# The seven products of a channel mixer: weights split in another order, additions moved between engines, and a reordered start

## The chip, the cores and the metric

The kernel runs on one core of a Trainium2 chip. The metric is the device time of one execution in microseconds; the median of several executions stands for a kernel. The engines are named as in the profile: PE is TensorE with its weight load PEld, DVE is VectorE, ACT is ScalarE, POOL is GpSimd, and SP is the engine whose queue issues most of the transfers.

## The reference, cut to what matters

Two layers work on a latent stream of 1024 tokens of width 1024. Layer 0 mixes tokens by a chunked gating, layer 1 by windowed attention, and each layer ends in a channel mixer with a convolution over the tokens:

```
def conv_ffn(h, w_up, conv_w, conv_b, w_down):          # h 1024 x 1024, w_up 1024 x 5632
    a, b = jnp.split(h @ w_up, 2, axis=-1)
    ap = jnp.pad(a, ((0, 0), (1, 1), (0, 0)))
    a = ap[:, :-2] * conv_w[0] + ap[:, 1:-1] * conv_w[1] + ap[:, 2:] * conv_w[2] + conv_b
    return (jax.nn.gelu(a) * b) @ w_down
...
        # last sublayer of layer i; sh2, sc2, g2 = columns of silu_c @ ada_w[i] + ada_b[i]
        h = modulate(rms_norm(x, norm_g[i, 2]), sh2, sc2)
        x = x + g2 * rms_norm(conv_ffn(h, f_w_up[i], f_conv_w[i], f_conv_b[i], f_w_down[i]), norm_g[i, 3])
```

All is float32. The change bears on the channel mixer of layer 1 and on the attention output that runs into it.

## The kernel before, in words

**One program, fixed orders.** The kernel is one program under a scheduler that fixes each engine's order of instructions when it is built. Work that belongs to different steps is mixed by Python generators: `step(gen)` lets a generator emit its next piece at that place in the program, and `tick()` does so for the norms that are pending.

**Split operands.** A float32 operand enters PE as two fp32r parts: ACT casts the source (tags `wh` for weights, `cmb` or `ah` for activations), and DVE subtracts the cast from the source (`wl`, `al`). One product of two operands is three matmuls: hi with hi, hi with lo, lo with hi. The tags `wh` and `wl` are rings of four buffers of 1024 columns, and `raw`, into which weights are loaded, is a ring of three. A buffer of a ring is written again only when its last reader has ended.

**The up-projection of layer 1** (`lat_ffn`, about 2237 to 2765 us of the trace). A job computes 128 columns f of the branch a and the same of b. It needs two weight blocks, `wa` and `wb`, each halved along the input channels: b11 and b21 are the halves of `wa`, b12 and b22 those of `wb`. The activations, in pairs of half-width groups (a11, a12, a21, a22), have been combined and split beforehand by `combine`. A job then has seven products instead of eight, with sums of weights t1 = b12 - b11, t2 = b22 - t1, t3 = b22 - b12 and t4 = b21 - t2, in three banks (X, Y, Z) of the product memory, in this order:

```
X  = a11 b11         -> s1 copied by ACT
Y  = s2 t2           -> b1 copied by ACT, then b1 + s1
Z  = s1 t1           -> s5 copied by ACT, then s5 + s1
Y += s3 t3           -> b2 copied by ACT        (Y holds s2 t2 + s3 t3)
X += a12 b21         -> left half of a copied by ACT
Z += s4 b22          -> DVE adds to b2 and b1
Y += a22 t4          -> right half of a, added by DVE
```

Y is used three times, so its fourth product (s3 t3) waits for the copy of b1 out of it. Below, P1 to P7 are these products in order. In a "full" job a product is 12 matmuls of 512 columns, in a "half" job (group g1) 12 of 256. After P7 `conv_gate` works on the finished job while PE is in the next: the first tap (POOL, `TENSOR_SCALAR row<-row,cwcols,lncols`), two more taps (DVE, `SCALAR_TENSOR_TENSOR row<-row,cwcols,row`), Gelu (ACT, `ACTIVATE row<-row`), a product with b, and the store.

Five "plain" jobs, which use only the first 512 tokens, come first, while the last two tiles of attention output are still being finished (`last_o`: eight weight blocks of `w_o`, 96 matmuls, then `late_norm` and transposes). Then come 17 full jobs with a half job after each third. During one job, `weights` loads, sums and splits the blocks of the next, one piece at each `step(more)`. A steady generator (`ada_steps`, one step after each full or half job) accumulates the gate of the sublayer in `lacc`, and its ninth step splits `lacc`, multiplies it by ones on PE in four matmuls and adds the bias.

The recording helper gives nearly every instruction of the trace the line L50, so rows are told apart by their tiles: `row` is a ring of work rows, `psA` and `psB` are product banks, `ident` the identity matrix of the transposes.

Of the kernel before, what the change touches and what calls it, by code (L numbers as in the profile page):

```python
# [15 lines left out]
P = 128  # L16
# [16 lines left out]
def hybrid_kernel(  # L33
# [79 lines left out]
    def psB(shape=(P, 512)):  # L113
        return ps.tile(list(shape), F32, name=nm("psB"), tag="psB", bufs=4)
# [71 lines left out]
    def ada_steps(l, m, streams, space=None):  # L186
# [11 lines left out]
        if m in (2, 5):  # L198
# [3 lines left out]
            for s, acc in zip(streams, accs):  # L202
                g = t_gate()
                hi, lo = (t_row(F32R), t_row(F32R)) if space else (t_w("wh"), t_w("wl"))
                S.copy(hi, acc)
                V.tensor_sub(lo, acc, hi)
                for h in range(2):
                    hs = slice(h * 512, (h + 1) * 512)
                    p = psB()
                    T.matmul(p, ones_r, hi[:, hs], start=True, stop=False)  # L210
                    T.matmul(p, ones_r, lo[:, hs], start=False, stop=True)
                    V.tensor_tensor(out=g[:, hs], in0=p, in1=bb[:, hs], op=ALU.add)
                V.tensor_tensor(out=g, in0=g, in1=ng, op=ALU.mult)
                gates[(l, m, s)] = g
# [682 lines left out]
    def lat_ffn(l, stage, n0, halos, gate, between, later):  # L897
# [60 lines left out]
        def weights(f, out, plain):  # L958
# [5 lines left out]
            def pair(src, names):  # L964
                n = src.shape[-1]
                hi, lo = t_w("wh"), t_w("wl")
                split_into((hi[:, 0:n], lo[:, 0:n]), src)
                for i, name in enumerate(names):
                    out[name] = [t[:, i * 512:(i + 1) * 512].rearrange("p (k n) -> p k n", n=P) for t in (hi, lo)]

            if plain:
                pair(wa, ("b11", "b21"))
                yield
                pair(wb, ("b12", "b22"))
                yield
                return
# [3 lines left out]
            pair(wa, ("b11", "b21"))  # L980
            yield
            G.tensor_tensor(out=t1, in0=b12, in1=b11, op=ALU.subtract)
            G.tensor_tensor(out=t2, in0=b22, in1=t1, op=ALU.subtract)
            V.tensor_sub(t4, b21, t2)
            pair(t24[:, 0:1024], ("t2", "t4"))
            yield
            G.tensor_tensor(out=t3, in0=b22, in1=b12, op=ALU.subtract)
            pair(t13[:, 0:1024], ("t1", "t3"))
            yield
            pair(b22, ("b22",))  # L990
# [4 lines left out]
        def conv_gate(f, a, N, b, where):  # L995
            c = t_row()[:, 0:N]
            G.tensor_scalar(out=c, in0=a[:, 1:1 + N], scalar1=cw[:, NF + f:NF + f + 1], scalar2=cb[:, f:f + 1],
                            op0=ALU.mult, op1=ALU.add)
# [46 lines left out]
        def up(f, groups, nxt):  # L1045
# [20 lines left out]
            def wide(t):  # L1066
                return t.rearrange("p (g n) -> p g n", n=256)

            X, Y, Z = psB(), psB(), psB()
            product(X, "a11", "b11", True)  # L1070
# [6 lines left out]
            G.tensor_tensor(out=b1, in0=b1, in1=wide(s1), op=ALU.add)  # L1077
# [3 lines left out]
            G.tensor_tensor(out=s5, in0=s5, in1=s1, op=ALU.add)  # L1081
# [3 lines left out]
            step(more)  # L1085
# [13 lines left out]
            step(more, 9)  # L1099
            product(Y, "a22", "t4", False)  # L1100
            V.tensor_tensor(out=av[:, :, 1, :], in0=wide(Y[:, 0:n]), in1=wide(s1), op=ALU.add)
            conv_gate(f, a, N, b, 512 * groups[0])

        for _ in combine(0):
            step(between, 2)
# [431 lines left out]
    def o_steps(tiles):  # L1537
# [34 lines left out]
        for i in range(nt):  # L1572
            active.append(post_norm(2, tiles[i], ys[i], gates[(1, 2, 0)], on_flip=on4, spare=tiles[0] >= 4, mod=(1, 3)))
            yield
# [72 lines left out]
    tail = last_o()  # L1647
    while not halos:
        step(tail)
    lat_ffn(1, 3, 5, halos, gate_of(1, 5), chain(tail, flushes(True)), lambda space: ada_steps(1, 5, (0,), space))  # L1650
# [43 lines left out]
```

## Time and profile before

| | |
|---|---|
| median of 3 executions | 3017.51 us (3013.89 to 3019.53) |
| profiled execution | 3020.14 us, its span 3018.2 us |
| PE busy | 2906.3 us, 96% of the span |
| DVE, ACT, POOL busy | 1878.1, 1197.6, 804.3 us |
| granted clock of PE, mean | 0.989 of full speed |

The span runs from the first to the last instruction of the profiled execution; its own time lies 1.9 us above the span and 2.6 us above the median. A granted clock of 1.00 is 2.4 GHz, of 0.5 it is 1.2 GHz.

### The profile page before, as it was taken

The page shows a single profiled execution, that of the slowest core. Times are in us where ns is not written, and L with a number is a line of the kernel's source. Part 1 is how long each engine was busy: PE and PEld are TensorE (multiplying, and loading weights), DVE is VectorE, ACT ScalarE, POOL GpSimd, SP SyncE. Part 2 cuts the span into 40 slices and gives each one's busy share as a digit, 9 for nine tenths or more (in the row PEclk, how much of TensorE's full clock was granted, in tenths as well). Part 3 has the DMA queues.
Part 4 walks back from the last instruction along what each step waited for, and adds up shares of the span by engine and source line. Part 5 has one row for each costly group of instructions (what it writes and reads, how often), then busy time and mean ns, then how long its engine had stood idle before and what let it go on. Part 6 is the DMA issues. An engine that isn't in the chain of part 4 may idle for free. (4 is left out here: it accounts for less than half of the span.)

```text
span 3018.2 us, 41884 instructions
## 1 busy us (share of the span) xinstructions
PE 2906.3 (96%) x16154; PEld 2567.7 (85%) x16154; DVE 1878.1 (62%) x2727; ACT 1197.6 (40%) x1979; POOL 804.3 (27%) x1046
## 2 busy tenths in 40 slices
PE   7999999999999999999999999899998998999999
PEld 5899888998999999899998877888888877777887
DVE  6557764756545555745454568897878676776333
ACT  4332242322432222432222334777785333333331
POOL 1151020710300001300011134564544453552000
PEclk9999999999999999999999999999998999999999
DMA  7754455532543233444355374266665332224642
GB/s 260 234 178 143 131 191 178 165 116 91 161 147 98 86 96 122 157 148 126 112 161 172 115 265 167 84 206 223 209 203 178 98 109 95 87 81 170 197 144 94
DMA packets 391096, 452.52 MB, mean 150 GB/s; under 512 B 15985, under 2 KB 291825, under 8 KB 390897
## 3 DMA queue, kind: packets, MB, share of 16 engines
q1 hardware_dynamic: 334481, 386.66, 40.2%
q10 hardware_dynamic: 55264, 58.99, 5.6%
q0 software_dynamic: 1152, 4.19, 0.4%
q8 instruction: 127, 2.08, 0.3%
q14 instruction: 72, 0.59, 0.1%
HBM read 367.73 MB, written 82.05 MB: 149 GB/s over the span
## 5 line engine op out<-in xcount | busy, mean ns | idle before, releaser
L50 PE MATMUL psA<-big,wh 128*128 128x320 f32 (+2 forms) x3840 | 729.8, 312 | 7.1 <-DVE tmp L50 3.5
L50 ACT CAST wh<-raw 128x1024 fp32r<-128x1024 f32 x344 | 350.9, 1022 | 759.2 <-PE psA L50 317.3
L50 PEld LDWEIGHTS psA<-big,wh 128*128 128x128 f32 x3840 | 607.9, 189 | 9.6 <-DVE tmp L50 4.4
L50 DVE TENSOR_TENSOR wl<-raw,wh 128x1024 fp32r<-128x1024 f32 x344 | 415.6, 1211 | 273.2 <-ACT wh L50 243.4
L50 PE MATMUL psB<-wh,act 128*128 128x512 f32 x1520 | 479.8, 395 | 2.3 <-DVE tmp L50 1.6
L50 PE MATMUL psA<-big,wl 128*128 128x322 f32 (+2 forms) x1920 | 441.4, 311 | 0.0
L50 PE MATMUL psB<-cmb,wh 128*128 128x512 f32 (+2 forms) x1352 | 374.2, 363 | 12.5 <-ACT row L50 9.7
L50 PEld LDWEIGHTS psB<-wh,act 128*128 128x128 f32 x1520 | 285.6, 188 | 69.7 <-issue 1.2
L50 PEld LDWEIGHTS psA<-big,wl 128*128 128x128 f32 x1920 | 323.8, 189 | 0.0
L50 PE MATMUL psB<-wl,act 128*128 128x512 f32 x760 | 299.6, 394 | 0.9 <-DVE wl L50 0.9
L50 PEld LDWEIGHTS psB<-cmb,wh 128*128 128x128 f32 x1352 | 242.0, 190 | 59.5 <-ACT row L50 16.8
L50 PE MATMUL psB<-wh,big 128*128 128x512 f32 x864 | 288.4, 401 | 2.6 <-ACT big L50 1.3
L50 PE MATMUL psB<-cmb,wl 128*128 128x512 f32 (+2 forms) x676 | 246.2, 364 | 9.6 <-DVE wl L50 9.6
L50 POOL TENSOR_SCALAR tmp<-tmp,cwcols,lncols 128x640 f32<-128x640 f32 (+1 forms) x44 | 65.1, 1480 | 702.4 <-ACT tmp L50 702.4
L50 DVE SCALAR_TENSOR_TENSOR acc<-raw,ccols,acc 128x1024 f32<-128x1024 f32 x119 | 150.6, 1286 | 159.9 <-DMA raw<-in_ada_w_dram 159.8
L50 PEld LDWEIGHTS psB<-wh,big 128*128 128x128 f32 x864 | 164.1, 191 | 40.9 <-ACT big L50 2.2
L50 POOL TENSOR_SCALAR sm<-sm 128x1 f32<-128x1 f32 (+1 forms) x76 | 34.9, 460 | 597.5 <-ACT tmp L50 317.2
L50 PEld LDWEIGHTS psB<-wl,act 128*128 128x128 f32 x760 | 142.8, 188 | 33.5 <-DVE wl L50 1.3
L50 PE MATMUL psB<-wl,big 128*128 128x512 f32 x432 | 167.6, 397 | 0.1
L50 POOL TENSOR_SCALAR row<-row,sm,sm 128x128 f32<-128x128 f32 x160 | 120.8, 769 | 149.0 <-DMA row<-vscr 143.4
L50 PEld LDWEIGHTS psB<-cmb,wl 128*128 128x128 f32 x676 | 128.5, 190 | 32.1 <-DVE wl L50 12.0
L50 DVE TENSOR_TENSOR y<-psB,y 128x512 f32<-128x512 f32 x140 | 95.9, 688 | 94.0 <-PE psB L50 92.8
(246 smaller groups left out, 4896.5 us busy)
## 6 DMA issues: line engine op xcount, KB each, us to landing
raw<-in_f_w_up_dram SPq DMA_DIRECT2D x142, 512.0 KB, 3.9
raw<-in_ada_w_dram SPq DMA_DIRECT2D x96, 512.0 KB, 4.2
raw<-in_a_w_in_dram SPq DMA_DIRECT2D x64, 512.0 KB, 4.7
wh<-woscr SPq DMA_DIRECT2D x48, 512.0 KB, 3.8
raw<-in_f_w_down_dram SPq DMA_DIRECT2D x44, 512.0 KB, 3.8
raw<-actd SPq DMA_DIRECT2D x44, 512.0 KB, 4.3
xT<-row ACTq DMA_DIRECT2D x33, 512.0 KB, 6.6
raw<-in_a_w_out_dram SPq DMA_DIRECT2D x32, 512.0 KB, 3.7
```

The lines of the kernel that those rows point to most:

```text
L50: ins = fn(*a, **kw)
```

## The change

The change does six things. (1) `weights` forms all four sums first, t1 and t3 on POOL, t2 and t4 on DVE, and then splits in the order of the products: b11 with t2, then t1 with t3, b21 with b22, and t4. The split columns are the same (3584 in a job), in six casts and six subtractions instead of four and four. (2) The additions b1 + s1 and s5 + s1 go from POOL to DVE, and t2 too. (3) The first tap of the convolution goes from POOL to ACT, as an Identity activation with scale and bias. (4) The places of `step(more)` in a job are moved. (5) The gate's matmuls with ones come a job later than the split of `lacc`, into `psA` instead of `psB`. (6) At the start, `combine(0)` is mixed one to one with `last_o` instead of following a run of it, and a `post_norm` loses its spare buffer.

```diff
@@ -204,9 +204,11 @@
                 hi, lo = (t_row(F32R), t_row(F32R)) if space else (t_w("wh"), t_w("wl"))
                 S.copy(hi, acc)
                 V.tensor_sub(lo, acc, hi)
+                if space:
+                    yield
                 for h in range(2):
                     hs = slice(h * 512, (h + 1) * 512)
-                    p = psB()
+                    p = (psA if space else psB)((P, 512))
                     T.matmul(p, ones_r, hi[:, hs], start=True, stop=False)
                     T.matmul(p, ones_r, lo[:, hs], start=False, stop=True)
                     V.tensor_tensor(out=g[:, hs], in0=p, in1=bb[:, hs], op=ALU.add)
@@ -961,41 +963,45 @@
                 Q.dma_start(w.rearrange("p (a b) -> p a b", a=KD),
                             w_up[l][:, col:col + P].rearrange("(k p) n -> p k n", p=P))
 
-            def pair(src, names):
-                n = src.shape[-1]
+            def pair(*parts):
                 hi, lo = t_w("wh"), t_w("wl")
-                split_into((hi[:, 0:n], lo[:, 0:n]), src)
-                for i, name in enumerate(names):
-                    out[name] = [t[:, i * 512:(i + 1) * 512].rearrange("p (k n) -> p k n", n=P) for t in (hi, lo)]
+                o = 0
+                for src, names in parts:
+                    n = src.shape[-1]
+                    split_into((hi[:, o:o + n], lo[:, o:o + n]), src)
+                    for i, name in enumerate(names):
+                        a = o + i * 512
+                        out[name] = [t[:, a:a + 512].rearrange("p (k n) -> p k n", n=P) for t in (hi, lo)]
+                    o += n
 
             if plain:
-                pair(wa, ("b11", "b21"))
+                pair((wa, ("b11", "b21")))
                 yield
-                pair(wb, ("b12", "b22"))
+                pair((wb, ("b12", "b22")))
                 yield
                 return
             t13, t24 = t_row(), t_row()
             b11, b21, b12, b22 = wa[:, 0:512], wa[:, 512:1024], wb[:, 0:512], wb[:, 512:1024]
             t1, t3, t2, t4 = t13[:, 0:512], t13[:, 512:1024], t24[:, 0:512], t24[:, 512:1024]
-            pair(wa, ("b11", "b21"))
+            G.tensor_tensor(out=t1, in0=b12, in1=b11, op=ALU.subtract)
+            V.tensor_sub(t2, b22, t1)
+            G.tensor_tensor(out=t3, in0=b22, in1=b12, op=ALU.subtract)
+            V.tensor_sub(t4, b21, t2)
             yield
-            G.tensor_tensor(out=t1, in0=b12, in1=b11, op=ALU.subtract)
-            G.tensor_tensor(out=t2, in0=b22, in1=t1, op=ALU.subtract)
-            V.tensor_sub(t4, b21, t2)
-            pair(t24[:, 0:1024], ("t2", "t4"))
+            pair((b11, ("b11",)), (t2, ("t2",)))
             yield
-            G.tensor_tensor(out=t3, in0=b22, in1=b12, op=ALU.subtract)
-            pair(t13[:, 0:1024], ("t1", "t3"))
+            pair((t13[:, 0:1024], ("t1", "t3")))
             yield
-            pair(b22, ("b22",))
+            pair((b21, ("b21",)), (b22, ("b22",)))
+            yield
+            pair((t4, ("t4",)))
             yield
 
         ahead = {}
 
         def conv_gate(f, a, N, b, where):
             c = t_row()[:, 0:N]
-            G.tensor_scalar(out=c, in0=a[:, 1:1 + N], scalar1=cw[:, NF + f:NF + f + 1], scalar2=cb[:, f:f + 1],
-                            op0=ALU.mult, op1=ALU.add)
+            S.activation(c, a[:, 1:1 + N], AF.Identity, bias=cb[:, f:f + 1], scale=cw[:, NF + f:NF + f + 1])
             V.scalar_tensor_tensor(out=c, in0=a[:, 0:N], scalar=cw[:, f:f + 1], in1=c, op0=ALU.mult, op1=ALU.add)
             V.scalar_tensor_tensor(out=c, in0=a[:, 2:2 + N], scalar=cw[:, 2 * NF + f:2 * NF + f + 1], in1=c,
                                    op0=ALU.mult, op1=ALU.add)
@@ -1067,6 +1073,7 @@
                 return t.rearrange("p (g n) -> p g n", n=256)
 
             X, Y, Z = psB(), psB(), psB()
+            step(more)
             product(X, "a11", "b11", True)
             s1 = t_s()[:, 0:n]
             S.copy(s1, X[:, 0:n])
@@ -1074,15 +1081,14 @@
             b = t_row()[:, 0:N]
             b1, b2 = [halves(b)[:, :, h, :] for h in range(2)]
             S.copy(b1, wide(Y[:, 0:n]))
-            G.tensor_tensor(out=b1, in0=b1, in1=wide(s1), op=ALU.add)
+            V.tensor_tensor(out=b1, in0=b1, in1=wide(s1), op=ALU.add)
             product(Z, "s1", "t1", True)
             s5 = t_s()[:, 0:n]
             S.copy(s5, Z[:, 0:n])
-            G.tensor_tensor(out=s5, in0=s5, in1=s1, op=ALU.add)
+            V.tensor_tensor(out=s5, in0=s5, in1=s1, op=ALU.add)
             step(more)
             product(Y, "s3", "t3", False)
             S.copy(b2, wide(Y[:, 0:n]))
-            step(more)
             product(X, "a12", "b21", False)
             a = t_row(shape=(P, 1028))
             av = halves(a[:, 1:1 + N])
@@ -1096,13 +1102,16 @@
             product(Z, "s4", "b22", False)
             V.tensor_tensor(out=b2, in0=b2, in1=wide(s5), op=ALU.add)
             V.tensor_tensor(out=b1, in0=wide(Z[:, 0:n]), in1=b1, op=ALU.add)
-            step(more, 9)
+            step(more)
             product(Y, "a22", "t4", False)
             V.tensor_tensor(out=av[:, :, 1, :], in0=wide(Y[:, 0:n]), in1=wide(s1), op=ALU.add)
+            step(more, 9)
             conv_gate(f, a, N, b, 512 * groups[0])
 
         for _ in combine(0):
-            step(between, 2)
+            step(between)
+        while n0 and not halos:
+            step(between)
         if n0:
             edge(halos[0])
         fill = chain(between, combine(1))
@@ -1570,7 +1579,7 @@
             for i in range(nt):
                 S.copy(ys[i][:, h * 512:(h + 1) * 512], pacc[:, i, :])
         for i in range(nt):
-            active.append(post_norm(2, tiles[i], ys[i], gates[(1, 2, 0)], on_flip=on4, spare=tiles[0] >= 4, mod=(1, 3)))
+            active.append(post_norm(2, tiles[i], ys[i], gates[(1, 2, 0)], on_flip=on4, mod=(1, 3)))
             yield
 
     halos = []
@@ -1644,10 +1653,8 @@
             active.append(late_norm(2, t, [acc[h][:, i, :] for h in range(2)], gates[(1, 2, 0)], (1, 3), on4))
             yield
 
-    tail = last_o()
-    while not halos:
-        step(tail)
-    lat_ffn(1, 3, 5, halos, gate_of(1, 5), chain(tail, flushes(True)), lambda space: ada_steps(1, 5, (0,), space))
+    tick()
+    lat_ffn(1, 3, 5, halos, gate_of(1, 5), chain(last_o(), flushes(True)), lambda space: ada_steps(1, 5, (0,), space))
     stage_pool["guard"].__exit__(None, None, None)
 
 
```

What that moves in the engines' orders is shown at three places. In the rows a name is a tag with two numbers of its buffer; `x2` is the same row twice.

ACT, in a full job that follows a full job, from the copy of s1 on. Before:

```order
L50 COPY s_3607_22799<-psB_3604_22784 128x512
L50 ACTIVATE row_3602_22774<-row_3602_22774 128x1024
L50 COPY row_3608_22813<-psB_3605_22785 128x2x256
L50 COPY s_3609_22828<-psB_3606_22786 128x512
L50 CAST wh_3614_22837<-raw_3610_22831 128x1024
L50 COPY row_3608_22813<-psB_3605_22785 128x2x256
L50 CAST wh_3616_22857<-row_3613_22836 128x1024
```

Of the change, from the first tap of the job that has ended:

```order
L50 ACTIVATE row_3604_22800<-row_3597_22755,lncols_645,cwcols1_731 128x1024
L50 COPY s_3613_22835<-psB_3606_22810 128x512
L50 ACTIVATE row_3604_22800<-row_3604_22800 128x1024
L50 COPY row_3614_22849<-psB_3607_22811 128x2x256
L50 CAST wh_3616_22867<-raw_3609_22813 128x512
L50 CAST wh_3616_22867<-row_3612_22818 128x512
L50 COPY s_3615_22864<-psB_3608_22812 128x512
```

The first tap stands ahead of the copy of s1, and the casts of b11 and t2 for the next job stand right behind the copy of b1, where before the next job's first cast (b11 and b21 together) followed the copy of s5. The Gelu (second row of before, third of the change) stands ahead of the copy of b1 in both.

DVE, in the passage from a half job to the full job behind it, from the addition that ends the half job's a. Before:

```order
L50 TENSOR_TENSOR row_3828_24260<-psB_3815_24172,s_3817_24186 128x256
L50 SCALAR_TENSOR_TENSOR row_3833_24300<-row_3828_24260,cwcols1_731,row_3833_24300 128x512 x2
L50 TENSOR_TENSOR row_3833_24300<-row_3833_24300,row_3818_24200 128x512
L50 TENSOR_TENSOR row_3843_24359<-raw_3840_24354,row_3843_24359 128x512
L50 TENSOR_TENSOR wl_3845_24361<-raw_3840_24354,wh_3844_24360 128x1024
L50 TENSOR_TENSOR row_3838_24336<-row_3838_24336,s_3839_24351 128x2x256
L50 TENSOR_TENSOR wl_3847_24381<-row_3843_24359,wh_3846_24380 128x1024
```

Of the change:

```order
L50 TENSOR_TENSOR row_3748_23765<-psB_3737_23678,s_3743_23702 128x256
L50 TENSOR_TENSOR wl_3754_23807<-row_3742_23685,wh_3753_23806 128x512
L50 SCALAR_TENSOR_TENSOR row_3755_23810<-row_3748_23765,cwcols1_731,row_3755_23810 128x512 x2
L50 TENSOR_TENSOR row_3762_23825<-raw_3760_23821,row_3761_23824 128x512
L50 TENSOR_TENSOR row_3755_23810<-row_3755_23810,row_3744_23716 128x512
L50 TENSOR_TENSOR row_3762_23825<-raw_3759_23820,row_3762_23825 128x512
L50 TENSOR_TENSOR row_3764_23856<-row_3764_23856,s_3763_23842 128x2x256
L50 TENSOR_TENSOR wl_3767_23875<-raw_3759_23820,wh_3766_23874 128x512
L50 TENSOR_TENSOR wl_3767_23875<-row_3762_23825,wh_3766_23874 128x512
L50 TENSOR_TENSOR s_3765_23871<-s_3765_23871,s_3763_23842 128x512
L50 TENSOR_TENSOR wl_3770_23910<-row_3761_23824,wh_3769_23909 128x1024
L50 TENSOR_TENSOR row_3764_23856<-row_3764_23856,s_3765_23871 128x2x256
```

Before, t4 (`row_3843`) and the first split for the next job (`wl_3845`, b11 and b21) came behind the taps and the product with b, and DVE had no addition of s1. In the change t2 and t4 (`row_3762`, twice) and the additions b1 + s1 (`row_3764`) and s5 + s1 (`s_3765`) stand among them, and the first split (`wl_3767`, twice) is in two pieces of 512 columns. The taps have 512 columns here because the job that ended is a half one.

DVE, in a full job behind a full job, from the addition that ends a. Of the change:

```order
L50 TENSOR_TENSOR row_3768_23905<-psB_3757_23818,s_3763_23842 128x2x256
L50 TENSOR_TENSOR wl_3774_23947<-row_3762_23825,wh_3773_23946 128x512
L50 SCALAR_TENSOR_TENSOR row_3775_23950<-row_3768_23905,cwcols1_731,row_3775_23950 128x1024
L50 TENSOR_TENSOR row_3782_23965<-raw_3780_23961,row_3781_23964 128x512
L50 SCALAR_TENSOR_TENSOR row_3775_23950<-row_3768_23905,cwcols1_731,row_3775_23950 128x1024
L50 TENSOR_TENSOR row_3782_23965<-raw_3779_23960,row_3782_23965 128x512
```

The two taps, which stood together before, are parted by t2 (`row_3782<-raw_3780,row_3781`), which needs t1 of POOL.

ACT, at the start, around the fifth weight block of `w_o`. Before (the casts `wh` are the fourth to sixth block):

```order
L50 CAST wh_3387_21172<-raw_3386_21170 128x1024
L50 ACTIVATE acc_3112_20025,sm_3339_21043<-row_3324_20988 128x1024
L50 DMA xs3_94<-row_3324_20988 128x1024
L50 ACTIVATE acc_3113_20026,sm_3340_21049<-row_3327_20995 128x1024
L50 DMA xs3_94<-row_3327_20995 128x1024
L50 CAST wh_3390_21190<-raw_3389_21188 128x1024
L50 CAST wh_3395_21218<-raw_3394_21216 128x1024
L50 ACTIVATE row_3347_21091<-psB_3348_21092,modc_83 128x128 x4
L50 ACTIVATE row_3347_21091<-psB_3349_21093,modc_83 128x128 x4
L50 ACTIVATE row_3350_21111<-psB_3351_21112,modc_83 128x128
```

Of the change (the cast `wh_3396` is the fifth block):

```order
L50 ACTIVATE row_3381_21124<-psB_3382_21125,modc_83 128x128
L50 ACTIVATE row_3381_21124<-psB_3383_21126,modc_83 128x128 x4
L50 ACTIVATE row_3384_21144<-psB_3385_21145,modc_83 128x128
L50 DMA xT3_98<-row_3381_21124 1024x1x128
L50 ACTIVATE row_3384_21144<-psB_3385_21145,modc_83 128x128 x3
L50 ACTIVATE row_3384_21144<-psB_3386_21146,modc_83 128x128 x4
L50 CAST cmb_3350_21053<-row_3376_21096 128x2x256
L50 DMA xT3_98<-row_3384_21144 1024x1x128
L50 CAST cmb_3346_21049<-row_3376_21096 128x2x256
L50 CAST cmb_3354_21057<-row_3377_21097 128x2x256
L50 CAST cmb_3358_21061<-row_3377_21097 128x2x256
L50 CAST wh_3396_21218<-raw_3395_21216 128x1024
```

The fifth block's cast, which stood ahead of the `ACTIVATE` rows that move the transposed tiles out of the banks, stands behind all 16 of them and behind seven `cmb` and `row` casts.

## Rows read from the trace of the kernel before

**Rows 1.** The page's engines: busy time, share, instructions.

```profile
PE 2906.3 (96%) x16154; PEld 2567.7 (85%) x16154; DVE 1878.1 (62%) x2727; ACT 1197.6 (40%) x1979; POOL 804.3 (27%) x1046
```

**Rows 2.** Windows: length, busy PE, PEld, DVE, ACT, POOL, PEclk, DMA, GB/s.

```profile
2237.00:2350.00 113.00, 97.75 (x630) 89.38 (x631) 85.99 (x98) 65.89 (x128) 49.90 (x50) 0.89 0.58 184
2237.00:2275.00 38.00, 31.28 (x130) 24.82 (x131) 27.63 (x38) 25.75 (x49) 12.82 (x14) 0.87 0.71 230
2350.00:2765.00 415.00, 389.23 (x1850) 319.44 (x1848) 289.98 (x249) 153.66 (x220) 194.61 (x171) 0.99 0.30 97
2450.00:2550.00 100.00, 91.43 (x417) 74.56 (x416) 69.30 (x60) 34.28 (x48) 44.78 (x40) 0.95 0.32 102
```

**Rows 3.** Waits of PE, 2350 to 2765: total, times, longest us.

```profile
PE psB L50 <- ACT row L50: 11.1, 19, 1.4
PE psB L50 <- DVE wl L50: 9.1, 5, 2.5
PE psB L50 <- DVE row L50: 4.1, 1, 4.1
```

**Rows 4.** PE's timeline: start us, us, instruction, idle before and releaser.

```profile
2393.55 0.62 PE L50 MATMUL psB<-cmb,wh 128*128 128x512 f32 x2
2394.00 0.40 PE L50 MATMUL psB<-cmb,wl 128*128 128x512 f32 x1
2394.71 0.50 PE L50 MATMUL psB<-cmb,wh 128*128 128x512 f32 x1 [0.31 <-ACT row L50]
...
2419.43 0.50 PE L50 MATMUL psB<-cmb,wl 128*128 128x512 f32 x1 [2.48 <-DVE wl L50]
...
2428.90 0.50 PE L50 MATMUL psB<-cmb,wh 128*128 128x512 f32 x1 [1.38 <-ACT row L50]
...
2522.44 0.80 PE L50 MATMUL psB<-row,ones 128*128 128x512 f32 x1 [4.10 <-DVE row L50]
```

**Rows 5.** Timelines of POOL, DVE and ACT beside a full job.

```profile
2387.01 1.50 POOL L50 TENSOR_SCALAR row<-row,cwcols,lncols 128x1024 f32<-128x1024 f32 x1 [7.75 <-ACT wh L50]
2388.49 1.29 POOL L50 TENSOR_TENSOR row<-raw,raw 128x512 f32<-128x512 f32 x1
...
2388.55 4.54 DVE L50 SCALAR_TENSOR_TENSOR row<-row,cwcols,row 128x1024 f32<-128x1024 f32 x2 [1.11 <-POOL row L50]
2393.02 1.27 DVE L50 SCALAR_TENSOR_TENSOR lacc<-raw,ccols,lacc 128x1024 f32<-128x1024 f32 x1
...
2393.13 1.06 ACT L50 ACTIVATE row<-row 128x1024 f32<-128x1024 f32 x1 [3.61 <-DVE row L50]
```

**Rows 6.** Groups by shape, 2350 to 2765: busy us, mean ns | idle before.

```profile
L50 POOL TENSOR_TENSOR row<-row,s 128x512 f32<-128x512 f32 x17 | 27.9, 1638 | 53.1 <-ACT row L50 53.1
L50 DVE TENSOR_TENSOR row<-row,s 128x512 f32<-128x512 f32 x17 | 11.5, 679 | 0.0
```

**Rows 7.** The page's DMA issues: count, KB each, us to landing.

```profile
raw<-in_f_w_up_dram SPq DMA_DIRECT2D x142, 512.0 KB, 3.9
...
xT<-row ACTq DMA_DIRECT2D x33, 512.0 KB, 6.6
```

**Rows 8.** Waits of PE, 2237 to 2350.

```profile
PE psA L50 <- DVE row L50: 4.0, 2, 2.7
PE psA L50 <- ACT row L50: 2.9, 1, 2.9
PE psA L50 <- POOL row L50: 2.5, 1, 2.5
PE psA L50 <- DVE wl L50: 2.5, 1, 2.5
PE psB L50 <- ACT cmb L50: 2.1, 1, 2.1
```

**Rows 9.** ACT's timeline at the transposed tiles.

```profile
2254.43 3.25 ACT L50 ACTIVATE row<-psB,modc 128x128 f32<-128x128 f32 x9 [2.16 <-PE psB L50]
```

**Rows 10.** PE's timeline at the start of the down-projection.

```profile
2765.63 0.51 PE L50 MATMUL psA<-wh,al 128*128 128x512 f32 x1 [2.05 <-DVE al L50]
```

## The prediction

> **What bounds the kernel now.** The page's engines come first: PE is busy for 2906.3 of 3018.2 us [rows 1], so time can only be won where PE waits or runs at the lower clock. The windows of the two stretches that the change touches come next [rows 2]. In the first, 2237 to 2350, PE is busy for 97.75 of 113 us at a granted clock of 0.89; the clock alone costs 0.11 x 113 = 12 us, of which 0.13 x 38 = 5 fall before 2275. In the second, 2350 to 2765, PE is busy for 389 of 415 us at 0.99, DVE for 290, POOL for 195, ACT for 154: no engine but PE is near its limit.
>
> The waits of PE in the second stretch then name what is late [rows 3]: 11.1 us for ACT's `row`, 9.1 us in five waits for DVE's `wl`, and one of 4.1 us for a DVE `row`; 24.3 us together. The timeline says where each stands [rows 4]. Two matmuls start 0.45 us apart, so one has 0.23 and a product of 12 has 2.77. The wait of 0.31 us is that of P4 for the copy of b1 in a full job behind a full job. The 2.48 us at 2419 are a half job's passage into a full one, where the split of the first weights is late; the 1.38 us at 2429 are P4 of the same full job. The 4.10 us are the gate's matmuls with ones, which wait for the split of `lacc`; just ahead of them stands one of the `ACT row` waits of 1.4, for the cast. In the 100 us around the gate the granted clock is 0.95 [rows 2], which is 0.05 x 100 = 5 us at full pace. So 24.3 us of waits and 5 of clock are what the second stretch can give.
>
> **The second stretch, part by part.** The terms go by one full job behind a full job, with 0 at its first matmul; P4 is due at 3 x 2.77 = 8.31.
>
> *The tap on ACT* takes 1.50 us from POOL's chain [rows 5]. No row shows an Identity of 1024 columns; the Gelu on as many took 1.06 us, and I take that. ACT was busy for 154 of 415 us, and 22 taps add about 20, so ACT carries it; the tap ends at about 1.9 after the addition that ends a (0.7) and the cast of t4. In the trace it ended at 2.4 on POOL.
>
> *The additions* b1 + s1 and s5 + s1 cost POOL 1.64 us each [rows 6]. The same shape with the same operand tags on DVE took 0.68 us. Both are wanted only after P6, at 16.6, by DVE itself, so PE doesn't see them. DVE gets 34 of 0.68 and 10 of about 0.41 (half jobs), t2 21 times 0.68 and some 6 us by the finer splits: some 47 us more, less what the taps no longer lose (next).
>
> *The taps on DVE.* Two took 4.54 us at 2388.55, while the same operation on `lacc` with nothing beside it took 1.27 [rows 5]. POOL's additions run beside the first, and 2 x 1.27 + 1.29 + a part of the next addition is about the 4.54 measured, as if the two engines took turns. After the change POOL has only t1 and t3 there, and I take 1.27 for a tap, plus what POOL's sums hold up. DVE's sum is then 290 + 47 - 25 = 312 of about 395 us: not a bound on average.
>
> *The Gelu and P4.* b1 is copied some 1.55 us after the Gelu begins (at 2393.13 [rows 5], and P4 goes on at 2394.71 [rows 4]), since the Gelu stands ahead on ACT as before. What decides is when the second tap ends. It stands behind t2, t2 behind t1 (POOL), t1 behind `wb`. The buffer of `wb` is free when b21 of the job before is subtracted; its cast writes a `wh` buffer that P6 reads until 16.6, so cast (0.62) and subtraction (0.68) end at about 18.0 and the load is issued there. At 3.9 us to landing [rows 7] `wb` is there at 21.9, which is 2.5 in the next job. The first tap runs from 1.9 to 3.15, t1 then to 4.4. Then t3 (POOL, 1.3), t2 (0.68) and the second tap (1.27) take turns, and the tap ends at about 7.5; b1 is copied at 9.05, and P4 waits about 0.75 us. The bounds are 0 (t3 behind the tap: 6.35, and b1 at 7.9) and 1.1.
>
> The Trainium skill says, under "SBUF — State Buffer", section "Who interferes with whom", that a VectorE instruction with two inputs in SBUF and a GpSimd one that reads SBUF exclude each other, the first one holding the ports until it ends. By that rule t2 on VectorE and t3 on GpSimd cannot overlap, and the wait is the 0.75; were they free of each other, it would be 0 and the sum 6 us better. The taps of 4.54 us for two speak for the rule.
>
> Eight of the eleven full jobs behind a full job have this order; in three (at the gate, and the last, which forms no sums) the Gelu stands free of t2, and the old 0.31 stays. That is 8 x 0.75 + 3 x 0.31 = 6.9 us.
>
> *The passages from half to full.* The first weights are now b11 (512 columns) and t2, formed and split early in the half job and not behind `lacc`'s step and the product with b. By the same chain b11's split is ready at about 10.5 where P1 wants it at about 10.5, so the five waits for `wl`, 9.1 us, go; the bound is 0.3 us for each. P4 waits 0.6 in the first two passages, where `lacc` still stands in DVE's order, and hardly in the others: 1.2 instead of about 1.4 each. In the half jobs the short products leave P6 or P7 waiting for a split, about 0.4 each, 2.0 in all.
>
> *The gate.* Its split comes a job before its matmuls, so 4.1 + 1.4 become at most 0.5, and with no wait of over 1 us left there I take the clock at full: 5 us become 0.5.
>
> Sum: waits 24.3 become 6.9 + 1.2 + 2.0 = 10.1, which with the 4.5 of clock makes 18.7 us less (8 with every wait at its upper bound and none of the clock, 26 with none left).
>
> **The first stretch.** The waits are 15.2 us [rows 8]. 4.2 of them lie before anything that moves (2.9 for ACT's `row`, 1.3 of DVE's) and stay. The waits for the combined operands and for weights between the plain jobs (2.1 for `cmb`, 2.5 for `POOL row`, 2.7 for `DVE row`, and 1.2 in small ones) go, since `combine(0)` is done before the first plain job and the transposes no longer stand between half-ready products. The price is on ACT: the fifth block of `w_o` is cast behind 16 activations and seven casts. Nine activations take 3.25 us [rows 9], 16 so 5.8, seven casts of some 0.6 another 4.2; the four blocks ahead give PE about 11 us, so the fifth waits some 3 us and the next 0.8, instead of the 2.5 for `wl` now. Waits: 4.2 + 3.8 = 8 instead of 15.2. The clock lost 5 before 2275 and 7 behind it; the new wait costs 1.5 more there, and the plain jobs, which then run nearly without a wait, get most of the 7 back: I take 5 net. Together 12 us less. Bounds: 3 (the clock stays low), 17 (no new wait).
>
> **The down-projection** begins with matmuls that wait 2.05 us for `al` [rows 10]. The last job's tap now stands on ACT ahead of the cast of the first `ah`: 1.06 at most, 0.8 taken, as a loss; bounds 0 and 2.
>
> **Sum.** 18.7 + 12 - 0.8 = 29.9. The profiled 3020.1 becomes 2990; with the median 2.6 lower, 2988.
>
> **The rivals.** (B) *VectorE is late in bursts.* DVE at 312 of 395 us has its splits, sums, taps and additions in one order; if in every full job two more of them come ahead of the second tap, its end goes to 8.3 and more, and P4 waits 1.5 us in eleven jobs, 16.5, with 8 more in the passages and half jobs. The second stretch then gives back nothing but the clock's 4.5, less if the waits lower it: 3020 - 12 - 4 + 1 = about 3005, and 3002 by the median. For it speaks the sum of DVE; against, that 80% of it is spread.
>
> (C) *The start gives nothing*: the fifth block is later than I think, and PE falls to the lower clock in between. The second stretch alone gives 18: 2999 to 3001. The granted clock of 0.87 in just this place [rows 2] speaks for it.
>
> (D) *The waits go altogether*: t3 lets the tap ahead, the half jobs have no wait. Then it is 26 + 15 less: about 2976.
>
> (E) *Slower: `wb` lands later.* The sums now stand ahead of everything in `weights` and need `wb`, which before was first wanted by t1 with b11 already split. Each microsecond that it lands later than 3.9 us is one more at P4, in the eight full jobs and at the five passages, 13 us in all. To lose the 30 and the 6 that can be told from no change (0.2% of 3017) takes 36 / 13 = 2.8 us, which is the 6.6 us that a transfer of the same size took elsewhere [rows 7]; the time is then about 3024. Against it: at a DMA share of 0.30 [rows 2] nothing crowds this stretch.
>
> **How the numbers follow.** My forecast (A, 2988, its own range 2979 to 2998) gets 0.57, B 0.14, C 0.14, D 0.09, E 0.06. The range from 2975 to 3006 holds A, C, D and most of B. Faster by over 0.2% are A, C, D and most of B, 0.88; within 0.2% the rest of B and half of E, 0.07; slower 0.05.
>
> **What would show it.** Right: the waits for `wl` at the passages gone; `ACT row` waits of some 0.7 us ahead of the fourth product in most full jobs; taps near 1.3 us; the matmuls with ones without a wait and the clock at 1.00 there; POOL's time in the second stretch down from 195 to about 65; one wait of some 3 us for a cast of `wh` between the `w_o` blocks, then plain jobs without waits. Wrong: waits of over 1.5 us in each full job, DVE busy over 350 us in the stretch, loads of `raw` that land after 5 us, or a granted clock below 0.9 still between 2275 and 2350.

## The result, and the profile after

The changed kernel takes 2996.33 us in the median of five executions (2989.85 to 2999.87), against 3017.51 for the kernel before (3010.94 to 3019.53, five); the ratio is 0.9933 [0.9915, 0.995]. That is 21 us less, where 30 were forecast.

The page's engines of the changed kernel, in its profiled execution of 2994.22 us (span 2992.4):

```profile
PE 2894.2 (97%) x16154; PEld 2556.0 (85%) x16154; DVE 1869.9 (62%) x2837; ACT 1229.7 (41%) x2050; POOL 667.4 (22%) x953
```

POOL lost 137 us of work and ACT gained 32 [rows 1]. To see where the time went, three stretches are measured on PE's timeline in each kernel: the start (from the end of the 2.9 us wait for ACT's `row` to the first matmul of 512 columns of the first full job), the jobs (from there to the end of the last product, or to the first matmul of the down-projection where that starts earlier), and the rest (to the end of the span). Before, these points lie at 2242.43, 2346.72, 2760.86 and 3018.2; after the change at 2237.51, 2338.26, 2734.22 and 2992.4.

| us | before | changed | difference | forecast |
|---|---|---|---|---|
| start | 104.3 | 100.8 | -3.5 | -12 |
| jobs | 414.1 | 396.0 | -18.2 | -18.7 |
| rest | 257.3 | 258.2 | +0.9 | +0.8 |

The three add up to 20.9 us, which is what the medians show. The two spans differ by 25.8: another 4.9 us lie ahead of 2237, in the part where both kernels give PE the same 12644 matmuls. Over all thirteen profiles of this document that part ends between 2235.7 and 2244.0, whatever the edits, so the 4.9 belong to these two executions and not to the change.

The waits of PE in the jobs (2338 to 2735), and in the start (2237 to 2338), as total, times and longest:

```profile
PE psB L50 <- ACT row L50: 9.5, 11, 1.3
PE psB L50 <- ACT s L50: 1.4, 5, 0.3
```

```profile
PE psA L50 <- ACT wh L50: 5.6, 2, 5.3
PE psA L50 <- DVE wl L50: 3.2, 2, 2.4
PE psA L50 <- ACT row L50: 2.9, 1, 2.9
PE psA L50 <- DVE row L50: 1.3, 1, 1.3
```

In the jobs the waits for `wl` and the gate's wait are gone and 24.3 us [rows 3] are 10.9. In the start 15.2 us [rows 8] are 13.0, and one wait of 5.3 us for ACT's cast of a `wh` is new. The windows of the two stretches and, between them, of 12 us that begin just before that wait ends (length, busy PE, PEld, DVE, ACT, POOL, granted clock, DMA, GB/s):

```profile
2237.50:2338.30 100.80, 90.41 (x603) 82.48 (x604) 73.76 (x89) 63.61 (x123) 33.29 (x38) 0.90 0.57 178
2258.00:2270.00 12.00, 8.42 (x20) 5.76 (x21) 10.53 (x13) 7.52 (x11) 3.08 (x3) 0.64 0.52 170
...
2338.30:2734.20 395.90, 384.98 (x1854) 317.93 (x1852) 288.24 (x360) 178.72 (x282) 70.10 (x87) 1.00 0.32 103
```

The jobs run at 1.00 now. The start's mean rose only from 0.89 [rows 2] to 0.90: in the 12 us about and behind the end of the 5.3 us wait, with the one of 2.4 among them, the mean is 0.64, so most of them are at the lower level, 1.2 GHz.

One P4 of a full job behind a full job, whose first matmul started at 2378.1, on POOL, DVE, ACT and PE (start us, us, instruction, idle before and what ended it):

```profile
2381.06 1.81 POOL L50 TENSOR_TENSOR row<-raw,raw 128x512 f32<-128x512 f32 x1 [17.42 <-DMA raw<-in_f_w_up_dram]
2382.83 1.32 POOL L50 TENSOR_TENSOR row<-raw 128x512 f32<-128x512 f32 x1
```

```profile
2380.41 1.28 DVE L50 SCALAR_TENSOR_TENSOR row<-row,cwcols,row 128x1024 f32<-128x1024 f32 x1 [0.82 <-issue]
2382.91 1.78 DVE L50 TENSOR_TENSOR row<-raw,row 128x512 f32<-128x512 f32 x1 [1.21 <-POOL row L50]
2384.62 1.27 DVE L50 SCALAR_TENSOR_TENSOR row<-row,cwcols,row 128x1024 f32<-128x1024 f32 x1
```

```profile
2385.93 1.06 ACT L50 ACTIVATE row<-row 128x1024 f32<-128x1024 f32 x1 [4.26 <-DVE row L50]
2386.89 0.57 ACT L50 COPY row<-psB 128x512 f32<-128x512 f32 x1
```

```profile
2387.51 0.73 PE L50 MATMUL psB<-cmb,wh 128*128 128x512 f32 x2 [0.96 <-ACT row L50]
```

The chain reads from the top: t1 starts on POOL at 2381.06, released by the load of `wb`, then t3 there and t2 on DVE in turn (t2 takes 1.78 us, an addition of the same shape took 0.68 [rows 6]), then the second tap, the Gelu, the copy of b1, and P4 goes on. The second tap ends 7.8 us after the job's start (7.5 forecast).

### The profile page after: what moved, and what is told of

It reads as the page before. It is cut to its first block, busy times and chain, and to the rows that moved or that the text cites. A ratio compares the mean times of both kernels' runs of the same rounds, so it can differ in the third digit from the quotient of the medians.

```text
span 2992.4 us, 41859 instructions
## 1 busy us (share of the span) xinstructions
PE 2894.2 (97%) x16154; PEld 2556.0 (85%) x16154; DVE 1869.9 (62%) x2837; ACT 1229.7 (41%) x2050; POOL 667.4 (22%) x953
## 5 line engine op out<-in xcount | busy, mean ns | idle before, releaser
L50 ACT CAST wh<-raw 128x1024 fp32r<-128x1024 f32 (+1 forms) x366 | 353.2, 973 | 735.2 <-PE psA L50 301.2
L50 DVE TENSOR_TENSOR wl<-raw,wh 128x1024 fp32r<-128x1024 f32 (+1 forms) x366 | 412.1, 1133 | 273.3 <-ACT wh L50 243.0
L50 PE MATMUL psB<-cmb,wh 128*128 128x512 f32 (+2 forms) x1352 | 371.1, 361 | 10.9 <-ACT row L50 9.5
```

What stands on the lines that cost most here:

```text
L50: ins = fn(*a, **kw)
```

## The experiments

The stretches and waits of every run's profile, measured in the same way; a median is given against that of the kernel before on the same chip. Each stretch is read from one profile. Kernels with the same instructions in their jobs agree within 1.2 us there (changed, x1 and x2 395.2 to 396.0; x9 and x10 385.4 and 385.6; x4, x8 and x11 379.8 to 381.0), so larger differences in that column belong to the edits.

| run | start | jobs | waits in the jobs | median us (before) | ratio |
|---|---|---|---|---|---|
| changed kernel | 100.8 | 396.0 | 10.9 | 2996.3 (3017.5) | 0.9933 [0.9915, 0.995] |
| x1 old start | 102.1 | 395.2 | 10.2 | 2998.4 (3012.4) | 0.9952 [0.9937, 0.9966] |
| x2 two blocks ahead | 99.0 | 395.3 | 10.1 | 2994.6 (3012.4) | 0.9939 [0.9923, 0.9955] |
| x3 t2 on GpSimd | 97.0 | 396.3 | 11.8 | 2994.6 (3012.4) | 0.9946 [0.9927, 0.9965] |
| x4 old pairs | 98.3 | 379.8 | 0 | 2976.1 (3012.4) | 0.9881 [0.9864, 0.9898] |
| x5 new pairs, old steps | 97.2 | 385.2 | 2.8 | 2986.7 (3016.0) | 0.9901 [0.9887, 0.9916] |
| x6 old pairs, tap on GpSimd | 100.7 | 401.7 | 15.9 | 2999.9 (3016.0) | 0.9949 [0.9934, 0.9963] |
| x7 old pairs, additions on GpSimd | 98.7 | 390.0 | 8.1 | 2990.1 (3016.0) | 0.9919 [0.9903, 0.9936] |
| x8 three more moves | 100.8 | 381.0 | 0.6 | 2984.8 (3016.0) | 0.9895 [0.9881, 0.991] |
| x9 before, tap and additions moved | 102.5 | 385.4 | 3.3 | 2990.1 (3018.0) | 0.9909 [0.9894, 0.9923] |
| x10 old pairs, old gate | 99.1 | 385.6 | 3.1 | 2986.7 (3018.0) | 0.9895 [0.9879, 0.9912] |
| x11 old pairs, last tap on GpSimd | 98.6 | 380.6 | 0.6 | 2980.7 (3018.0) | 0.988 [0.9862, 0.9897] |

**x4, the sums, pairs and places of step(more) as before**, t2 on GpSimd with them, and the other edits kept (the lines with `step(more)` as in the kernel before):

```diff
-            G.tensor_tensor(out=t1, in0=b12, in1=b11, op=ALU.subtract)
-            V.tensor_sub(t2, b22, t1)
-            G.tensor_tensor(out=t3, in0=b22, in1=b12, op=ALU.subtract)
-            V.tensor_sub(t4, b21, t2)
-            yield
-            pair((b11, ("b11",)), (t2, ("t2",)))
...
+            pair(wa, ("b11", "b21"))
+            yield
+            G.tensor_tensor(out=t1, in0=b12, in1=b11, op=ALU.subtract)
+            G.tensor_tensor(out=t2, in0=b22, in1=t1, op=ALU.subtract)
+            V.tensor_sub(t4, b21, t2)
+            pair(t24[:, 0:1024], ("t2", "t4"))
+            yield
+            G.tensor_tensor(out=t3, in0=b22, in1=b12, op=ALU.subtract)
+            pair(t13[:, 0:1024], ("t1", "t3"))
+            yield
+            pair(b22, ("b22",))
...
```

> The changed kernel with the sums, the pairs of splits and the places of step(more) as before (edits 1 and 4 undone; t2 on GpSimd); additions on VectorE, tap on ACT, gate a job later and the new start stay. If the new pairing is what removed the waits for the first weights: the passages from half to full wait 1.3 to 2.5 us for DVE's wl again, some 9 us, less the 5 us that the gate's clock does not lose, and the jobs take 396 + 5 to 9 = 401 to 405. If the lighter chain behind a job (tap on ACT, no additions on GpSimd) was enough by itself: 396 to 399, and P4's waits of 0.9 go as well, since t2 is then out of VectorE's order.

Neither size was right: the jobs have no wait at all, and PE is busy in every one of their microseconds (window of its jobs):

```profile
2342.30:2722.00 379.70, 379.70 (x1854) 318.07 (x1852) 291.69 (x296) 178.95 (x246) 115.01 (x108) 1.00 0.34 107
```

So the tap, the additions and the gate were enough in the jobs, and the new sums and pairs, with their places and with t2 on VectorE, take 16.2 us back. 379.8 us is what the products take without a wait. The changed kernel's 16 waits, 10.9 us by the list, go with 16.2. Most of the difference is in how a wait is listed: its idle time counts from the end of the matmul before, whose row is 0.40 us long, while without a wait the next starts 0.23 us after that one's start, which leaves out 0.17 us for each wait. And the first two matmuls behind a wait take 0.73 us (row at 2387.51) where such a pair takes 0.62 [rows 4], another 0.11. The two make some 4.5 of the 5.3 us; the rest was not followed.

**x5, only the places of step(more) undone** (new sums and pairs, so that the sums come after P3):

> The changed kernel with its sums first and its new pairs (edit 1), but step(more) at the places of before (edit 4 undone), so that the sums come after P3 and not at the job's start; t2 on VectorE. If the 16 us that the old pairs won come from where the sums stand (beside the taps, waiting for wb) and not from what is paired with what: the waits of 0.9 us ahead of P4 go, and the jobs take 380 to 384 us. If the pairing itself or the finer splits cost it: 390 to 396, with waits in the same places as in the changed kernel or for wl in the passages.

```profile
PE psB L50 <- ACT row L50: 2.8, 6, 0.9
```

The jobs take 385.2, a little above the first range: of the 16.2 us, 10.7 come from the places of `step(more)`, and 5.5 from the sums and pairs themselves and t2 on VectorE. Five of the six waits left stand ahead of P4 in the full jobs behind half jobs, and one of 0.6 behind the gate; in the other full jobs behind full jobs the waits of 0.9 us are gone. x5 moves the splits together with the sums, so it doesn't say alone that it is the sums' place that counts; x3, next, takes t2 alone out of VectorE's order, and the same waits go.

**x3, t2 on GpSimd in the changed kernel** (`V.tensor_sub(t2, b22, t1)` becomes `G.tensor_tensor(out=t2, in0=b22, in1=t1, op=ALU.subtract)`):

> The changed kernel with t2 formed on GpSimd, as before, behind t1; t4 stays on VectorE. If P4 waits because the second tap stands behind t2, which waits for t1 and so for the load of wb: the taps run without it, the second ends at about 6.0 after the job's start instead of 7.7, the waits of 0.9 us ahead of P4 in the full jobs behind full jobs go, PE's waits in the jobs fall from 10.9 to about 4, and the jobs take about 390 us instead of 396. If it is VectorE's load as such or the order on ACT, the 0.9 us stay. GpSimd's t2 of 1.3 to 2.3 us could hold up the taps: then 393.

```profile
PE psB L50 <- ACT s L50: 9.6, 5, 2.0
PE psB L50 <- ACT row L50: 2.2, 4, 0.6
```

The waits ahead of P4 in the full jobs behind full jobs went, all but one of 0.6 us, as forecast, so t2 on VectorE ahead of the second tap is their cause. But the jobs take 396.3: each of the five half jobs now waits 1.9 us at P6 for ACT's copy of s5, where the changed kernel waits 0.3 (its `ACT s` waits), which neither expectation had named, and the gain is lost there.

**x6 and x7, from x4, the tap or the additions back on GpSimd:**

```diff
-            S.activation(c, a[:, 1:1 + N], AF.Identity, bias=cb[...], scale=cw[...])          (x6)
+            G.tensor_scalar(out=c, in0=a[:, 1:1 + N], scalar1=cw[...], scalar2=cb[...], op0=ALU.mult, op1=ALU.add)
-            V.tensor_tensor(out=b1, ...)  V.tensor_tensor(out=s5, ...)                        (x7)
+            G.tensor_tensor(out=b1, ...)  G.tensor_tensor(out=s5, ...)
```

> The kernel with the old pairs (which had no wait in its jobs, 379.8 us), the first tap back on GpSimd: of the moves only the additions on VectorE, the gate and the start are left. If the tap on ACT carries the gain: the Gelu comes late again, P4 waits 0.3 us in full jobs and 1.4 behind half jobs, and the jobs take 390 to 400. If taking the additions off GpSimd was enough: 380 to 384.

> The kernel with the old pairs, the additions b1 + s1 and s5 + s1 back on GpSimd: tap on ACT, gate and start are left. If the additions carry the gain, because GpSimd's 1.6 us instructions make VectorE's wait: the passages wait for wl again, 1.3 to 2.5 us each, and the jobs take 388 to 395. If the tap on ACT was enough: 380 to 384.

Waits of x6, then of x7, in the jobs:

```profile
PE psB L50 <- ACT row L50: 12.4, 20, 1.4
PE psB L50 <- DVE wl L50: 3.5, 5, 1.4
```

```profile
PE psB L50 <- DVE wl L50: 5.4, 5, 1.7
PE psB L50 <- ACT row L50: 2.8, 5, 0.8
```

The tap is worth 22 us when the additions are on VectorE, the additions 10 when the tap is on ACT. Both bring back the waits for `wl` in the passages, without any change in the pairing. x7's 390.0 lies in its first range, x6's 401.7 above its range of 390 to 400.

**x9, the kernel before with only the tap and the two additions moved:**

> The kernel before with nothing but the first tap on ACT and the two additions on VectorE: old sums and pairs, old gate, old start. If these moves alone take the waits out of the jobs: only the gate's wait of 4 to 5.5 us and its clock of some 3 us stay, the jobs take 384 to 389 us instead of 414.1, the start 102 to 104, and the whole is about 25 us faster than before and 4 us or more faster than the changed kernel. If the new pairing was needed for the passages: waits for wl there, jobs of 395 or more, no faster than the changed kernel.

```profile
PE psB L50 <- ACT row L50: 3.3, 2, 3.1
```

Jobs of 385.4: these three moved instructions give 28.7 of the 34.4 us between 414.1 and the 379.8 without a wait. The one long wait left is the gate's. How they reach the first weights is seen on DVE in a half job, in the passage where before PE waited 2.48 us for `wl` [rows 4]: from t4 over the step on `lacc` and the product with b to the first split for the next job. Before, then x9:

```profile
2413.65 0.69 DVE L50 TENSOR_TENSOR row<-raw,row 128x512 f32<-128x512 f32 x1 [1.20 <-POOL row L50]
2414.26 2.31 DVE L50 SCALAR_TENSOR_TENSOR lacc<-raw,ccols,lacc 128x1024 f32<-128x1024 f32 x1
2416.49 1.75 DVE L50 TENSOR_TENSOR row<-row,row 128x1024 f32<-128x1024 f32 x1
2418.17 1.21 DVE L50 TENSOR_TENSOR wl<-raw,wh 128x1024 fp32r<-128x1024 f32 x1
```

```profile
2407.38 0.68 DVE L50 TENSOR_TENSOR row<-raw,row 128x512 f32<-128x512 f32 x1
2407.98 1.27 DVE L50 SCALAR_TENSOR_TENSOR lacc<-raw,ccols,lacc 128x1024 f32<-128x1024 f32 x1
2409.18 1.21 DVE L50 TENSOR_TENSOR row<-row,row 128x1024 f32<-128x1024 f32 x1
2410.32 1.21 DVE L50 TENSOR_TENSOR wl<-raw,wh 128x1024 fp32r<-128x1024 f32 x1
```

The half job's first matmul started at 2405.87 before and at 2401.24 in x9, so the split ends 13.5 us into the job before and 10.3 in x9. In x9 t4 doesn't wait for GpSimd's sum, and the two DVE instructions behind it, beside which GpSimd then has no work left, take 2.48 us instead of 4.06.

The whole is 27.8 us faster than before (25 expected). Its ratio of 0.9909 lies below the changed kernel's 0.9933, with intervals that overlap; the jobs, 10.5 us shorter in the profiles, tell the two apart.

**x10, from x4, the gate as before:**

> The kernel with the old pairs (jobs 379.8, no wait) with the gate's matmuls as before, in the step of their split and in psB. If the gate cost what the kernel before showed: one wait of 4.1 us and one of 1.4, the clock below 1.00 for some 10 us behind them, and jobs of 385 to 389. If the split comes early enough once VectorE is relieved: one wait of 1 to 2 us, and 381 to 384.

```profile
2498.41 0.73 PE L50 MATMUL psB<-row,ones 128*128 128x512 f32 x2 [3.05 <-ACT row L50]
```

385.6 instead of 379.8: the gate's later matmuls are worth 5.8 us, of which 3.05 are this wait of the matmuls with ones for ACT's cast of `lacc`; the wait of 4.1 for DVE [rows 3] was gone already. The time is that of the first expectation (385 to 389), with one wait in place of its two. x9 has the same gate: its 28.7 and these 5.8 us make up the 34.4, and nothing is left that the new pairing would have to give.

**x1 and x2, the start.** x1 undoes edit 6; x2 puts two blocks of `w_o` ahead of the pending norms (x2's edit):

```diff
-    tick()
-    lat_ffn(..., chain(last_o(), flushes(True)), ...)
+    tail = last_o()
+    step(tail, 2)
+    lat_ffn(..., chain(tail, flushes(True)), ...)
```

> The changed kernel with the start (edit 6) as before. If the parts simply add: the start, from the end of PE's 2.9 us wait to the first full job, takes 104.3 us again instead of 100.8, the full and half jobs stay at 396.0, and the kernel is 3.5 us slower than the changed one. If the start's reordering pays only with the other edits, or they with it, the jobs' 396.0 moves too, by more than 2 us.

> The changed kernel, but two blocks of w_o are issued before the pending norms are ticked, so that the fifth and sixth cast stand on ACT ahead of the 16 activations of the transposed tiles; combine(0) stays mixed one to one. If the start falls short of the forecast because of where the fifth block's cast stands on ACT: the waits of 5.3, 2.4 and 0.3 us there shrink to under 3 together, the granted clock between 2232 and 2270 rises from 0.77 to 0.85 or more, and the start takes 100.8 - 6 = about 94 us (93 to 97). If the clock is low there whatever ACT does, or another wait takes their place: 99 to 102.

x1's jobs didn't move by 2 us, so the start adds by itself. Its size is uncertain: one profile each of three kernels with the old start shows 104.3, 102.1 and 102.5 us, and of eight with the new one (without x2 and x8) 97.0 to 100.8, so it is worth 1 to 7 us, some 4 between the means (103.0 and 98.8). x2 left 0.8 of the 5.3 us wait, but its 99.0 lies within those 97.0 to 100.8, so no gain is shown; its second expectation, that another wait takes the place, came. The longest of its waits in the start, and the window around them:

```profile
PE psA L50 <- DVE wl L50: 3.6, 2, 3.3
PE psA L50 <- DVE row L50: 3.6, 2, 2.2
```

```profile
2260.00:2278.00 18.00, 12.42 (x41) 8.95 (x39) 17.82 (x22) 13.39 (x23) 5.78 (x4) 0.81 0.52 156
```

DVE is busy for 17.82 of 18 us there, and the wait of 3.3 us is now one for its split.

**x8 and x11, on top of x4.** x11 puts the last job's first tap on GpSimd; x8 does that, adds x2's edit, and forms s2 and s4 of `combine(0)` on GpSimd.

> The kernel with the old pairs, and three more moves: the last job's first tap on GpSimd, so that ACT casts the down-projection's first operand at once; two blocks of w_o ahead of the norms; and s2 and s4 of combine(0) on GpSimd, since VectorE was busy for 17.8 of 18 us there. The jobs stay at 379.8. The wait of 3.06 us at the down-projection should go or fall under 1, 2 us less. If VectorE is what holds the start back: the start takes 94 us instead of 97 to 101; if GpSimd's slower subtractions take its place: 98 to 103. In all 2970 to 2976 against a median of before of 3012 to 3017.

> The kernel with the old pairs, and the last job's first tap on GpSimd, nothing else. The down-projection's first matmuls wait for al 2.06 us as before instead of 3.06 for ah; the jobs stay at 379.8, and the whole is 1 us less than with the old pairs alone, 2973 to 2977. If the difference is lost in the clock behind the wait, nothing changes.

The wait for `ah` of 3.06 us became one of 2.06 for `al` in x8, as before, but neither kernel is faster than x4: 0.9895 and 0.988 against 0.9881, and both medians, 2984.8 and 2980.7, lie above what was expected of them. In x8 the start took 100.8, which is what its expectation gave for GpSimd's slower subtractions taking VectorE's place. It doesn't settle whether VectorE holds the start back, since VectorE was not relieved (window of x8):

```profile
2260.00:2278.00 18.00, 11.63 (x40) 8.42 (x38) 17.99 (x16) 12.46 (x22) 11.85 (x7) 0.81 0.60 195
```

With two subtractions fewer DVE is busy for 17.99 of the 18 us, with 16 instructions where x2 had 22, and POOL for 11.85 instead of 5.78. PE again waits 3.9 us for ACT's cast and 3.6 for a split. What bounds the start stays open. x4 and x11 are the best versions measured, and can't be told apart.

## Why the prediction was right, and where not

The time lies in the range and the direction is right; the sum missed by 9 us, in the start.

*The jobs, 18.7 forecast, 18.2 measured.* The chain to P4 came as worked out: `wb` 3.0 us into the job (2.5), the second tap's end at 7.8 (7.5), and eight P4 waits of 0.9 to 1.3 and one of 0.6 in the full jobs behind full jobs, 8.5 us, against eight of 0.75 and 6.9 with the rest. The passages wait 1.0 (1.2), the half jobs 1.4 (2.0), the gate not at all, with the clock at 1.00. That t2 on DVE and t3 on POOL took turns is borne out: 1.78 us for a t2 that began while t3 ran. The Trainium skill's rule in "SBUF — State Buffer", section "Who interferes with whom", which was weighed for this, agrees with that row. Rival B (VectorE late in bursts) didn't come: DVE was busy for 288 of 396 us, not 312, mainly since its taps fell by 34.6 us where 25 were counted. The 32 long ones, before and after, in the jobs:

```profile
L50 DVE SCALAR_TENSOR_TENSOR row<-row,cwcols,row 128x1024 f32<-128x1024 f32 x32 | 67.4, 2107 | 18.3 <-POOL row L50 17.7
L50 DVE SCALAR_TENSOR_TENSOR row<-row,cwcols,row 128x1024 f32<-128x1024 f32 x32 | 42.8, 1339 | 13.0 <-issue 7.4 <-ACT row L50 5.4
```

Rival E (`wb` lands later) didn't come either: the weight loads of the jobs took 4.1 us in the median, not 6.6.

*The ceiling was read too low.* "So 24.3 us of waits and 5 of clock are what the second stretch can give" takes a wait at the idle time listed for it. x4, without a wait, gives 34.4, more than the 26 that were kept for the case with none left.

*The tap on ACT* took 1.24 us and not the Gelu's 1.06, and PE doesn't wait for it: with the tap on ACT x4's jobs have no wait at all. The Trainium skill, "ScalarE: Activation LUTs", section "What ACT_TABLE_LOAD costs", gives about 93 ns more for each of scale and bias that is a pointer to a column; two of these make an estimate of 0.19 us by that page, against the 0.18 between the two, so the agreement is close, and the page would have given the right price.

*The reason given for the passages was not what they needed, so that their number was right is in part luck.* The prediction let the waits for `wl` go because "the first weights are now b11 (512 columns) and t2, formed and split early". x9 and x4 show that they go without that, with the tap and the additions alone, and that on top of these the new pairing with its sums at the job's start is a loss of 16.2 us. Whether the pairing would also have removed them by itself is not shown: no run has it with the tap and the additions left on GpSimd. The prediction let the tap take "1.50 us from POOL's chain", and of the additions it said that "PE doesn't see them"; x9 shows that together they are most of the gain, 28.7 us.

*The start* is the step that failed: "Waits: 4.2 + 3.8 = 8 instead of 15.2", and "I take 5 net" for the clock. ACT's timeline of the changed kernel, from the first activation of the transposed tiles to the cast of the fifth block, and PE's transposes, the last matmul of the fourth block and the first two of the fifth:

```profile
2246.74 1.16 ACT L50 ACTIVATE row<-psB,modc 128x128 f32<-128x128 f32 x3 [3.95 <-PE psB L50]
...
2256.65 1.14 ACT L50 CAST cmb<-row 128x512 fp32r<-128x512 f32 x2 [1.06 <-POOL row L50]
2257.69 1.04 ACT L50 CAST wh<-raw 128x1024 fp32r<-128x1024 f32 x1
```

```profile
2246.04 1.91 PE L50 MATMUL psB<-ident,acc 128*128 128x128 f32 x16
...
2253.09 0.40 PE L50 MATMUL psA<-wh,row 128*128 128x512 f32 x1
2258.79 1.22 PE L50 MATMUL psA<-wh,row 128*128 128x512 f32 x2 [5.30 <-ACT wh L50]
```

The order was as forecast, and the run ahead of the cast took 10.9 us, the 10 us of the forecast and a wait of 1.06 for POOL. What failed is the overlap: "the four blocks ahead give PE about 11 us". ACT's run begins with PE's transposes, for which it waited 3.95 us, and two of the four blocks stand ahead of these on PE; the other two, 24 matmuls from 2247.71 to 2253.49, are only 5.8 us. So PE waited 5.3 us and not 3, and 2.4 more for the next `wl` where 0.8 were forecast. This is no chance of one execution: in the eight kernels with this start (x2 and x8 left out) the two waits are 4.0 to 5.3 and 1.9 to 2.4 us. In all, waits of 13.0 remained, which is 2.2 us won for 7.2, and the granted clock of 0.64 for 12 us took back most of what the plain jobs won at 1.00: by the means of 0.89 and 0.90 some 1.5 us were won for 5. That is nearly rival C, at 2999 to 3001.

*The down-projection* lost 0.9 (0.8). The wait at its first matmuls grew from 2.05 us [rows 10] to 3.06, as worked out; but the rest as a whole takes 255.9 to 259.6 us over the thirteen profiles, so that it comes so near to the forecast is luck.

## What to carry to other kernels

When several edits work on one chain, ask of each what it gives once the others are in: here two moves of small instructions off GpSimd took the waits away, and a rearrangement meant for the same waits put a load and a GpSimd sum ahead of an activation that PE waits for. A sum that depends on a transfer should not be issued on the engine, and at the place, of the chain that the next product waits for. When one engine's work is to cover another's, count only what stands behind the point from which the other can begin: here that was two blocks and not four. And moving one wait of a start in which three engines hand work to each other gained nothing that could be told from the spread.

## What the runs showed of the hardware that was not expected

A short wait of PE cost more than the idle time listed for it: 16 waits listed at 10.9 us went with 16.2, and the busy time of PE in the jobs was 385.0 us instead of x4's 379.7 for the same number of matmuls, at a granted clock of 1.00 in both. An engine can get more instructions and finish its chain sooner: with three instructions moved off GpSimd the step on `lacc` in a passage took 1.27 us on VectorE instead of 2.31. And the Identity with scale and bias from columns took 1.24 us on 1024 columns where Gelu took 1.06.
